# Score pairs first in the scheduling order, turned weights in small rotating tiles, a third raw weight buffer

## Chip, cores and metric

One core of a Trainium2 chip runs the kernel. The metric is the device time of one execution in microseconds; the number to predict is the median of the runs of the changed kernel.

## What is computed

Two transformer blocks of two layers each, one after the other, in float32, on 512 tokens of width 1024. The first block's layer has two attention mixers on one input projection, gates, an output projection, and a gated feed-forward with a short convolution. The second block has a chunked linear attention, a differential attention, a Fourier mixer and a gated feed-forward, on the tokens and on 256 context tokens. The change touches the first block's two mixers in code, and the weight loads of everything.

```python
# mixer A, per head: windows in three groups of heads (dilation 1, 4, 16)
scores = einsum(q, k) * hd ** -0.5 + alibi bias, masked
p = exp(scores - max);  o = (p @ v) / sum(p)
# mixer B (stick-breaking), per block of 128 queries
z = einsum(q_blk, k) * hd ** -0.5
log_stay = where(causal, log_sigmoid(-z), 0)
later = reverse_cumsum(log_stay) - log_stay
o = where(causal, exp(log_sigmoid(z) + later), 0) @ v
```

Heads have 64 dimensions. Mixer A has three groups of four heads, mixer B four heads.

## The kernel before, in words

The program is traced in Python through a tile framework. Each engine gets its instructions in an order that a planner fixes when the program is built: it takes what is ready by its own time model, the earliest in program order first. Tiles come from pools with a number of buffers for each tag; who wants a buffer that is still in use waits for its last reader.

**Weights.** `weights` (line 106) hands out a weight and asks for the one that the next call will want. `load_weights` (line 116) takes, for each 128 x 1024 piece, a raw tile (pool "raw", two buffers, line 55), a high-half tile (three buffers) and a low-half tile (two), issues the load on the SP queue (line 125), casts raw to the high half on ACT (line 126) and subtracts it from raw on DVE (line 127). So a raw buffer is free when the subtraction is done. Every projection (`mm3`, lines 133 to 135) is three matmuls a piece: high by high, high by low, low by high. A piece feeds 24 matmuls of 512 columns for the tokens, or of 256 columns for the context or half the tokens.

**The two mixers of the first block** (`mixer1`): q, k and v are projected; then for j = 0 and 1 `stick` (line 541) and `dsw` (line 472) are traced, then the joining of the groups, 16 gate projections, and the output. The planner puts matmuls of the gate projections between the attention's.

A head pair shares tiles: head 0 has partitions 0 to 63 of q and k, head 1 has 64 to 127, and each has its own bank in a score tile `sc` of two banks (one such tile).

- `stick`, for each of four query blocks: scores of the pair (line 553, 128 to 512 columns), tanh on ACT (555), mask, stay factors, two scans and a product on DVE (557 to 565), `turned`, then the value products (570). There the two heads write different halves of the partitions of `po`.
- `dsw`, for each of four blocks: scores for three groups of heads (line 488), bias and maximum on DVE (494) and exp on ACT (496) for each head and half, `turned`, the value products (505), and copies of sums (508, 509).
- `turned` (line 459) turns the weights of both heads by 128 x 128 transposes into one tile `at` of two banks (line 467) and copies them to SBUF by `evac`: head 0 on ACT (line 785), head 1 on DVE (line 783). The target is one pair tile `pT` with one buffer.

`self.tmp` gives tiles of 128 x 512 from the pool "tmp" with four buffers; the first block uses it before attention (squares of x) and after it (joining, merging, feed-forward).

Of the kernel before, what the change touches and what calls it, by code (L numbers as in the profile page):

```python
# [18 lines left out]
P = 128  # L19
# [11 lines left out]
class Split:  # L31


    def __init__(self, hi, lo):
        self.hi, self.lo = hi, lo
# [12 lines left out]
class Net:  # L48
    def __init__(self, ctx, tc, io, plan):
        self.plan, self.asked, self.ahead = plan, [], []  # L50
        self.tc, self.nc, self.io = tc, tc.nc, io
        pool = lambda name, bufs, **kw: ctx.enter_context(tc.tile_pool(name=name, bufs=bufs, **kw))
        self.pc = pool("const", 1)
        self.px = pool("resid", 1)
        self.praw = pool("raw", 2)
        self.pw = pool("wsplit", 1)
        self.ps = pool("tmp", 4)
        self.psm = pool("small", 4)
        self.n = 0
        self.consts()  # L60
# [398 lines left out]
    def turned(self, t, n):  # L459

        nc = self.nc
        pt = self.pair_bank("at")
        pT = self.pair_tile("pT")
        for i in range(2):
            for k in range(n):
                sl = slice(k * P, (k + 1) * P)
                nc.tensor.transpose(pt[:, i, sl], t[:, i, sl], self.ident)
        for i in range(2):
            self.evac(i, pT[:, i, :n * P], pt[:, i, :n * P])
        return pT  # L470

    def dsw(self, j, qa, ka, va, sums, stat):

        nc = self.nc
        bias = self.pair_tile("bias")
        nc.sync.dma_start(bias, self.io["dswb"][2 * j:2 * j + 2].rearrange("s p c -> p s c"))
        for b in range(4):
            k0 = max(b - 1, 0) * P  # L480
            n0 = (b + 1) * P - k0
            own = slice(b * P, (b + 1) * P)
            ps = self.pair_bank("sc")
            for g, cols, keys in ((0, slice(0, n0), slice(k0, (b + 1) * P)), (1, slice(n0, n0 + P), own),
                                  (2, slice(n0 + P, n0 + 2 * P), own)):
                for i in range(2):
                    r = slice(64 * i, 64 * i + 64)
                    nc.tensor.matmul(ps[:, i, cols], qa[2 * g + j][r, own], ka[2 * g + j][r, keys], start=True, stop=True)
            e = self.pair_tile("y", 2)
            for i in range(2):  # L490
                s = 2 * j + i
                for c, (sl, bi) in enumerate(((slice(0, n0), slice(256 - n0, 256)), (slice(n0, n0 + 2 * P), slice(256, 512)))):
                    nm = stat[:, c, b, 0, s:s + 1]
                    nc.vector.tensor_tensor_reduce(e[:, i, sl], ps[:, i, sl], bias[:, i, bi], -1.0, 3.0e38, ALU.add, ALU.min,
                                                   accum_out=nm)
                    nc.scalar.activation(e[:, i, sl], e[:, i, sl], AF.Exp, bias=nm, scale=-1.0)
            n = n0 // P + 2
            pT = self.turned(e, n)
            po = self.bank("po")
            for i in range(2):  # L500
                s = 2 * j + i
                vs = [(0, va[0][k0 // P + k][:, s, :]) for k in range(n - 2)]
                vs += [(1, va[1][b][:, 4 * (g - 1) + s, :]) for g in (1, 2)]
                for k, (c, v) in enumerate(vs):
                    nc.tensor.matmul(po[:, 130 * i + 65 * c:130 * i + 65 * (c + 1)], pT[:, i, k * P:(k + 1) * P], v,  # L505
                                     start=k in (0, n - 2), stop=k in (n - 3, n - 1))
            po = po[:, 0:260].rearrange("p (s c d) -> p c s d", s=2, c=2)
            nc.scalar.copy(sums[b][:, :, 2 * j:2 * j + 2, :], po[:, :, :, 0:64])
            nc.vector.tensor_copy(stat[:, :, b, 1, 2 * j:2 * j + 2], po[:, :, :, 64])
# [31 lines left out]
    def stick(self, j, qb, kb, vb):  # L541

        nc = self.nc
        po = self.bank("po")
        for qi in range(4):
            kw = (qi + 1) * P
            pz = self.pair_bank("sc")  # L550
            for i in range(2):
                r = slice(64 * i, 64 * i + 64)
                nc.tensor.matmul(pz[:, i, :kw], qb[j][r, qi * P:kw], kb[j][r, 0:kw], start=True, stop=True)
            y = self.pair_tile("y", 2)
            nc.scalar.activation(y[:, :, :kw], pz[:, :, :kw], AF.Tanh, scale=0.5)
            d = y[:, :, qi * P:kw]
            nc.vector.tensor_tensor(d, d, self.smask.unsqueeze(1).broadcast_to([P, 2, P]), ALU.min)

            g = self.pair_tile("stay")
            nc.gpsimd.memset(g[:, :, 0:1], 1.0)  # L560
            nc.vector.tensor_scalar(g[:, :, kw - 1:0:-1], y[:, :, 1:kw], -0.5, 0.5, ALU.mult, ALU.add)
            for i in range(2):
                c = g[:, i, 0:kw]
                nc.vector.tensor_tensor_scan(c, c, c, 1.0, ALU.mult, ALU.bypass)
            nc.vector.scalar_tensor_tensor(y[:, :, :kw], y[:, :, :kw], 1.0, g[:, :, 0:kw][:, :, ::-1], ALU.add, ALU.mult)
            pT = self.turned(y, qi + 1)
            for k in range(qi + 1):
                for i in range(2):
                    h = 2 * j + i
                    nc.tensor.matmul(po[64 * i:64 * i + 64, qi * P:kw], vb[:, k, h * 64:(h + 1) * 64], pT[:, i, k * P:(k + 1) * P],  # L570
                                     start=k == 0, stop=k == qi, tile_position=(0, 64 * i))
        o = self.pv.tile([P, T], F32, tag=f"ob{j}", name=self.nm("ob"))
        nc.scalar.copy(o, po)
        return o
# [1111 lines left out]
```

## Time and profile before

| | us |
|---|---|
| median of three runs | 3280.42 |
| lowest and highest run | 3278.43, 3285.65 |
| the profiled execution | 3286.37 |
| its span, first to last instruction | 3284.6 |
| PE busy in it | 3200.1 |
| DVE, ACT busy in it | 2000.4, 1350.6 |

PE is TensorE's matmul, DVE is VectorE, ACT is ScalarE, SP the engine that issues most loads. A busy PE is not a PE at its peak: matmuls are pipelined, so a record lasts longer than the distance from one start to the next. A float32 matmul shows as two records, a projection matmul as one. "mm<-h,whi" names what an instruction writes and reads. A row of the timeline merges consecutive records of one line and operation and shows their count; the time in it runs from the start of the first to the end of the last. What stands behind an arrow is the instruction that ended the idle time before.

### The profile page before, as it was taken

Reading aid. Unit: us, or ns where it says so; the run is one execution under the profiler, and the core shown is the slowest. Engines: PE = TensorE matmul, PEld = TensorE weight load, DVE = VectorE, ACT = ScalarE, POOL = GpSimd, SP = SyncE. Lnnn points to the kernel's source line nnn. Section 1 sums busy time; section 2 is a strip of 40 time slices with the busy share of each in tenths; the row PEclk is TensorE's granted clock in tenths of the full one; section 3 lists DMA queues with packets and bytes.
Section 4 is the critical chain, followed back from the end, with each engine's and each line's share of the span. In section 5 each row is a group of like instructions: output and inputs, shape, how many; then the busy total and the mean of one; then the engine's idle time right before and its main releaser. Section 6 shows DMA issues by size and latency. Waiting matters only on the chain.

```text
span 3284.6 us, 46618 instructions
## 1 busy us (share of the span) xinstructions
PE 3200.1 (97%) x18792; PEld 2674.0 (81%) x18792; DVE 2000.4 (61%) x3256; ACT 1350.6 (41%) x2246; POOL 68.8 (2%) x197
## 2 busy tenths in 40 slices
PE   9999999999999999999999999999999999999997
PEld 7778887888778887888778788888898778888887
DVE  4456799663556899567767765333266677652335
ACT  3243432242243423346647644222235467542223
POOL 0000000000000000000100000000000100000000
PEclk9999999999999999999999999999999999999999
DMA  4213466432223566344332134332134522223333
GB/s 133 84 40 119 145 199 209 124 103 91 70 81 94 162 210 199 118 133 151 101 115 70 58 118 133 93 99 85 58 117 128 166 77 70 78 78 96 96 96 116
DMA packets 109159, 370.59 MB, mean 113 GB/s; under 512 B 13200, under 2 KB 18320, under 8 KB 108944
## 3 DMA queue, kind: packets, MB, share of 16 engines
q1 hardware_dynamic: 103760, 352.28, 35.0%
q0 software_dynamic: 5184, 15.34, 1.6%
q8 instruction: 147, 2.41, 0.3%
q14 instruction: 68, 0.56, 0.1%
HBM read 359.64 MB, written 7.93 MB: 112 GB/s over the span
## 4 chain that ended last, share of the span: by engine, by line
PE 73%; DVE 11%; DMA 10%; ACT 4%; issue 1%; ACTq 0%; SPq 0%; DVEq 0%
PE mm L135 19%; PE mm L133 19%; PE mm L134 19%; DVE wlo L127 3%; DMA raw<-w_up 3%; ACT whi L126 2%; DVE junk L689 2%; DMA raw<-w_fi 2%; DMA wmod<-w_mod 1%; DVE wmod L689 1%; PE at L1273 1%; DMA raw<-w_in2t 1%; DMA raw<-w_fo 1%; PE po L505 1%; DMA raw<-w_in2v 1%
## 5 line engine op out<-in xcount | busy, mean ns | idle before, releaser
L126 ACT CAST whi<-raw 128x1024 fp32r<-128x1024 f32 (+1 forms) x556 | 576.0, 1036 | 1282.3 <-PE mm L134 282.7
L127 DVE TENSOR_TENSOR wlo<-raw,whi 128x1024 fp32r<-128x1024 f32 (+1 forms) x556 | 667.2, 1200 | 364.2 <-PE mm L135 170.7
L133 PE MATMUL mm<-h,whi 128*128 128x512 f32 x1904 | 753.0, 396 | 13.6 <-ACT whi L126 6.9
L135 PE MATMUL mm<-h,wlo 128*128 128x512 f32 x1904 | 753.6, 396 | 1.1 <-DVE wlo L127 0.9
L134 PE MATMUL mm<-h,whi 128*128 128x512 f32 x1904 | 751.0, 394 | 0.0
L133 PEld LDWEIGHTS mm<-h,whi 128*128 128x128 f32 x1904 | 358.8, 188 | 88.3 <-ACT whi L126 10.0
L135 PEld LDWEIGHTS mm<-h,wlo 128*128 128x128 f32 x1904 | 358.5, 188 | 79.9 <-DVE wlo L127 7.3
L134 PEld LDWEIGHTS mm<-h,whi 128*128 128x128 f32 x1904 | 358.7, 188 | 72.6 <-issue 2.8
L135 PE MATMUL mm<-hid,wlo 128*128 128x512 f32 (+1 forms) x896 | 325.7, 364 | 4.0 <-DVE wlo L127 3.7
L133 PE MATMUL mm<-hid,whi 128*128 128x512 f32 (+1 forms) x896 | 324.4, 363 | 1.8 <-ACT whi L126 1.8
L134 PE MATMUL mm<-hid,whi 128*128 128x512 f32 (+1 forms) x896 | 324.1, 362 | 0.9 <-DVE hid L180 0.9
L135 PEld LDWEIGHTS mm<-hid,wlo 128*128 128x128 f32 x896 | 168.0, 188 | 35.3 <-DVE wlo L127 7.6
L133 PEld LDWEIGHTS mm<-hid,whi 128*128 128x128 f32 x896 | 168.0, 188 | 29.7 <-ACT whi L126 2.0
L134 PEld LDWEIGHTS mm<-hid,whi 128*128 128x128 f32 x896 | 168.1, 188 | 29.0 <-DVE hid L180 1.4
L133 PE MATMUL mm<-cat,whi 128*128 128x512 f32 (+1 forms) x512 | 185.9, 365 | 3.2 <-ACT cat L716 2.7
L135 PE MATMUL mm<-cat,wlo 128*128 128x512 f32 (+1 forms) x512 | 186.2, 364 | 0.2 <-DVE wlo L127 0.2
L134 PE MATMUL mm<-cat,whi 128*128 128x512 f32 (+1 forms) x512 | 185.7, 363 | 0.0
L1414 DVE TENSOR_TENSOR silu<-silu,mm 128x512 f32<-128x512 f32 (+1 forms) x58 | 36.1, 623 | 221.6 <-PE mm L135 221.1
L689 DVE SCALAR_TENSOR_TENSOR junk<-wmod,c 128x1024 f32<-128x1024 f32 x96 | 116.8, 1217 | 4.2 <-DMA wmod<-w_mod 3.7
L689 DVE SCALAR_TENSOR_TENSOR wmod<-wmod,c 128x1024 f32<-128x1024 f32 x96 | 116.8, 1217 | 0.7
L133 PEld LDWEIGHTS mm<-cat,whi 128*128 128x128 f32 x512 | 96.2, 189 | 18.8 <-ACT cat L716 2.9
L135 PEld LDWEIGHTS mm<-cat,wlo 128*128 128x128 f32 x512 | 96.4, 189 | 15.4 <-DVE wlo L127 0.4
(491 smaller groups left out, 5119.5 us busy)
## 6 DMA issues: line engine op xcount, KB each, us to landing
raw<-w_fi SPq DMA_DIRECT2D x120, 512.0 KB, 3.6
wmod<-w_mod SPq DMA_DIRECT2D x96, 512.0 KB, 4.2
raw<-w_up SPq DMA_DIRECT2D x88, 512.0 KB, 3.7
raw<-w_in2t SPq DMA_DIRECT2D x76, 512.0 KB, 3.7
raw<-w_in_t SPq DMA_DIRECT2D x64, 512.0 KB, 3.6
raw<-w_fo SPq DMA_DIRECT2D x48, 512.0 KB, 3.5
raw<-w_down SPq DMA_DIRECT2D x32, 512.0 KB, 3.7
raw<-w_out SPq DMA_DIRECT2D x28, 512.0 KB, 3.6
```

What stands on the lines that cost most here:

```text
L126: nc.scalar.copy(hi, raw)
L127: nc.vector.tensor_tensor(lo, raw, hi.bitcast(F32), ALU.subtract)
L133: mm(out, lh, rh, start=start, stop=False)
L134: mm(out, lh, rl, start=False, stop=False)
L135: mm(out, ll, rh, start=False, stop=stop)
L505: nc.tensor.matmul(po[:, 130 * i + 65 * c:130 * i + 65 * (c + 1)], pT[:, i, k * P:(k + 1) * P], v, start=k in (0, n - 2), stop=k in (n - 3 ...
L689: ins = nc.vector.scalar_tensor_tensor(o, w, 1.0, cs[v], ALU.mult, ALU.mult, accum_out=self.mods[l][v][:, j:j + 1])
L1273: mm(po[:, 0:64], wT[:, i * P:(i + 1) * P], vals[c0 + i][:, h * 64:(h + 1) * 64], start=c0 + i == 0, stop=c0 + i == nkb - 1)
L1414: nc.vector.tensor_tensor(s, s, ps[1][:, :n], ALU.mult)
```

## The change

Three edits. The score matmuls in `stick` and `dsw` are traced inside `high_priority()`, which gives them the priority of the program's start, so that the planner takes them before anything else that is ready. `turned` copies each head's turned weights into a tile of its own from `tmp`; the value products of `stick` take head 1 before head 0. The raw pool has three buffers.

```diff
--- before.py
+++ after.py
@@ -52,7 +52,7 @@
         pool = lambda name, bufs, **kw: ctx.enter_context(tc.tile_pool(name=name, bufs=bufs, **kw))
         self.pc = pool("const", 1)
         self.px = pool("resid", 1)
-        self.praw = pool("raw", 2)
+        self.praw = pool("raw", 3)
         self.pw = pool("wsplit", 1)
         self.ps = pool("tmp", 4)
         self.psm = pool("small", 4)
@@ -460,13 +460,13 @@
 
         nc = self.nc
         pt = self.pair_bank("at")
-        pT = self.pair_tile("pT")
+        pT = [self.tmp("pT") for _ in range(2)]
         for i in range(2):
             for k in range(n):
                 sl = slice(k * P, (k + 1) * P)
                 nc.tensor.transpose(pt[:, i, sl], t[:, i, sl], self.ident)
         for i in range(2):
-            self.evac(i, pT[:, i, :n * P], pt[:, i, :n * P])
+            self.evac(i, pT[i][:, :n * P], pt[:, i, :n * P])
         return pT
 
     def dsw(self, j, qa, ka, va, sums, stat):
@@ -483,9 +483,10 @@
             ps = self.pair_bank("sc")
             for g, cols, keys in ((0, slice(0, n0), slice(k0, (b + 1) * P)), (1, slice(n0, n0 + P), own),
                                   (2, slice(n0 + P, n0 + 2 * P), own)):
-                for i in range(2):
-                    r = slice(64 * i, 64 * i + 64)
-                    nc.tensor.matmul(ps[:, i, cols], qa[2 * g + j][r, own], ka[2 * g + j][r, keys], start=True, stop=True)
+                with self.tc.high_priority():
+                    for i in range(2):
+                        r = slice(64 * i, 64 * i + 64)
+                        nc.tensor.matmul(ps[:, i, cols], qa[2 * g + j][r, own], ka[2 * g + j][r, keys], start=True, stop=True)
             e = self.pair_tile("y", 2)
             for i in range(2):
                 s = 2 * j + i
@@ -502,7 +503,7 @@
                 vs = [(0, va[0][k0 // P + k][:, s, :]) for k in range(n - 2)]
                 vs += [(1, va[1][b][:, 4 * (g - 1) + s, :]) for g in (1, 2)]
                 for k, (c, v) in enumerate(vs):
-                    nc.tensor.matmul(po[:, 130 * i + 65 * c:130 * i + 65 * (c + 1)], pT[:, i, k * P:(k + 1) * P], v,
+                    nc.tensor.matmul(po[:, 130 * i + 65 * c:130 * i + 65 * (c + 1)], pT[i][:, k * P:(k + 1) * P], v,
                                      start=k in (0, n - 2), stop=k in (n - 3, n - 1))
             po = po[:, 0:260].rearrange("p (s c d) -> p c s d", s=2, c=2)
             nc.scalar.copy(sums[b][:, :, 2 * j:2 * j + 2, :], po[:, :, :, 0:64])
@@ -548,9 +549,10 @@
         for qi in range(4):
             kw = (qi + 1) * P
             pz = self.pair_bank("sc")
-            for i in range(2):
-                r = slice(64 * i, 64 * i + 64)
-                nc.tensor.matmul(pz[:, i, :kw], qb[j][r, qi * P:kw], kb[j][r, 0:kw], start=True, stop=True)
+            with self.tc.high_priority():
+                for i in range(2):
+                    r = slice(64 * i, 64 * i + 64)
+                    nc.tensor.matmul(pz[:, i, :kw], qb[j][r, qi * P:kw], kb[j][r, 0:kw], start=True, stop=True)
             y = self.pair_tile("y", 2)
             nc.scalar.activation(y[:, :, :kw], pz[:, :, :kw], AF.Tanh, scale=0.5)
             d = y[:, :, qi * P:kw]
@@ -565,9 +567,9 @@
             nc.vector.scalar_tensor_tensor(y[:, :, :kw], y[:, :, :kw], 1.0, g[:, :, 0:kw][:, :, ::-1], ALU.add, ALU.mult)
             pT = self.turned(y, qi + 1)
             for k in range(qi + 1):
-                for i in range(2):
+                for i in (1, 0):
                     h = 2 * j + i
-                    nc.tensor.matmul(po[64 * i:64 * i + 64, qi * P:kw], vb[:, k, h * 64:(h + 1) * 64], pT[:, i, k * P:(k + 1) * P],
+                    nc.tensor.matmul(po[64 * i:64 * i + 64, qi * P:kw], vb[:, k, h * 64:(h + 1) * 64], pT[i][:, k * P:(k + 1) * P],
                                      start=k == 0, stop=k == qi, tile_position=(0, 64 * i))
         o = self.pv.tile([P, T], F32, tag=f"ob{j}", name=self.nm("ob"))
         nc.scalar.copy(o, po)
```

## Rows read from the trace of the kernel before

**Rows 1.** Part 1 of the page: busy time, share of the span and instructions of each engine.
```profile
PE 3200.1 (97%) x18792; PEld 2674.0 (81%) x18792; DVE 2000.4 (61%) x3256; ACT 1350.6 (41%) x2246; POOL 68.8 (2%) x197
```
**Rows 2.** Windows: stretch, busy us (xinstructions) by engine, granted clock, DMA share, GB/s.
```profile
145.00:235.00 90.00, 88.07 (x543) 62.67 (x542) 54.92 (x138) 36.89 (x72) 3.84 (x11) 1.00 0.11 33
866.00:956.00 90.00, 87.90 (x536) 62.37 (x535) 54.58 (x138) 36.89 (x72) 2.98 (x9) 0.98 0.11 32
1930.00:2010.00 80.00, 76.55 (x611) 73.69 (x609) 63.65 (x95) 43.93 (x65) 0.00 (x0) 0.98 0.50 152
2050.00:2100.00 50.00, 50.00 (x222) 41.36 (x221) 16.79 (x20) 14.73 (x20) 0.00 (x0) 1.00 0.31 95
```
**Rows 3.** Groups by line, 145 to 235 us: busy us, mean ns, then idle before and releaser.
```profile
L488 PE MATMUL sc<-qk,qk 64*128 64x128 f32 (+1 forms) x96 | 14.4, 334 | 0.0
L494 DVE CUSTOM_DVE_ANT_0 y<-sc,bias 128x256 f32<-128x256 f32 (+1 forms) x32 | 11.4, 401 | 7.3 <-PE sc L488 7.3
L553 PE MATMUL sc<-qk,qk 64*128 64x128 f32 (+3 forms) x32 | 10.8, 482 | 0.3 <-ACT y L555 0.3
L783 DVE COPY pT<-at 128x512 f32<-128x512 f32 (+3 forms) x16 | 9.1, 570 | 14.8 <-ACT pT L785 14.7
L570 PE MATMUL po<-pT,vb 128*64 128x128 f32 x80 | 8.7, 286 | 0.7 <-DVE pT L783 0.5
```
**Rows 4.** Timeline of PE, 145 to 201 us: start, us, operation, merged records.
```profile
145.98 0.49 PE L553 MATMUL sc<-qk,qk 64*128 64x128 f32 x4
...
149.26 0.70 PE L553 MATMUL sc<-qk,qk 64*128 64x256 f32 x4 [0.29 <-ACT y L555]
...
152.56 0.44 PE L570 MATMUL po<-pT,vb 128*64 128x128 f32 x4
...
152.92 0.91 PE L553 MATMUL sc<-qk,qk 64*128 64x384 f32 x2
...
155.33 1.12 PE L553 MATMUL sc<-qk,qk 64*128 64x512 f32 x2
...
156.38 0.66 PE L570 MATMUL po<-pT,vb 128*64 128x128 f32 x8
...
160.53 0.43 PE L570 MATMUL po<-pT,vb 128*64 128x128 f32 x2
...
191.97 0.92 PE L553 MATMUL sc<-qk,qk 64*128 64x384 f32 x4
...
199.90 0.94 PE L488 MATMUL sc<-qk,qk 64*128 64x128 f32 x12
```
**Rows 5.** Waits of PE, whole run: line, releaser, us in total, times, longest us.
```profile
PE mm L135 <- DVE wlo L127: 12.8, 27, 1.1
PE mm L133 <- ACT whi L126: 12.7, 6, 6.9
PE mm L171 <- DVE wlo L127: 3.5, 5, 0.8
PE mm L153 <- DVE wlo L127: 2.1, 1, 2.1
PE mm L170 <- ACT whi L126: 1.5, 3, 0.8
PE sc L553 <- ACT y L555: 0.7, 2, 0.4
```
**Rows 6.** Timeline of DVE, 1946 to 1957 us.
```profile
1949.12 1.22 DVE L127 TENSOR_TENSOR wlo<-raw,whi 128x1024 fp32r<-128x1024 f32 x1 [0.80 <-ACT whi L126]
...
1955.14 1.22 DVE L127 TENSOR_TENSOR wlo<-raw,whi 128x1024 fp32r<-128x1024 f32 x1 [0.30 <-ACT whi L126]
```
**Rows 7.** Timeline of PE in the same stretch.
```profile
1950.98 0.28 PE L133 MATMUL mm<-KK,whi 128*128 128x256 f32 x1
...
1951.33 0.28 PE L133 MATMUL mm<-KK,whi 128*128 128x256 f32 x1
```
**Rows 8.** DMA issues: count, size of one, median us from issue to landing.
```profile
raw<-w_fi SPq DMA_DIRECT2D x120, 512.0 KB, 3.6
```

## The prediction

> **What bounds the kernel now.** I read the share of busy time first: PE is busy 97% of the span, DVE 61%, ACT 41% [rows 1]. So whatever does not shorten the instruction stream of PE, or remove a moment in which PE stands, is worth nothing. Busy is no throughput, though, so the windows come next [rows 2]. In a dense projection stretch (2050 to 2100 us) PE runs 222 matmuls of 512 columns in 50 us, one every 0.225 us, without a gap and at the full granted clock; nothing in this change touches that rate, and dense stretches make up most of the kernel. Two kinds of stretch differ.
>
> The first kind is attention in the two layers of the first block, 145 to 235 us and 866 to 956 us. PE is busy 88.07 and 87.90 of 90 us there, DVE 54.9 and 54.6, so PE is the bound [rows 2]. But what PE does is wasteful. The scores of two heads lie in the two halves of the partitions (0 to 63 and 64 to 127). Where both matmuls of a pair stand next to each other, the timeline shows them running at the same time: four records of 384 columns take 0.92 us, while two records of one head alone take 0.91 us [rows 4]. Many pairs are torn apart by transposes or value products of the step before, which come earlier in the program and so win as soon as they are ready. Then each half pays the full price.
>
> The second kind is where the weight chain is late: the second block's stages that work on 256 columns, 1930 to 2010 us for one, where PE is busy 76.55 of 80 us [rows 2]. The waits of PE say what it stands for: the high or low half of a weight [rows 5].
>
> **The change part by part.**
>
> *Score pairs with priority.* No instruction is added or removed; the order on PE's queue changes. I take what each line costs PE now in one attention stretch and what it would cost with every pair whole, from the merged records [rows 3, 4]. Stick-breaking scores (L553): four sizes per half, paired 0.49 + 0.70 + 0.92 + 1.12 = 3.23 us (the last is the row of one head, since at 384 columns one and two cost the same), twice 6.46; now 10.8, so 4.3 us less. Window scores (L488): three pairs of 128 columns take 0.94 us, and a block whose first pair has 256 columns takes 0.21 more (0.70 less 0.49), so 2 x (0.94 + 3 x 1.15) = 8.8; now 14.4, so 5.6 us less. Value products of the stick part (L570) use two column halves in the same way; the loop order (1, 0) starts with the head that DVE evacuates last, so that a pair is not begun with one member. Two records of one head and four of both cost the same there, 0.43 and 0.44 us, eight take 0.66 [rows 4]: with 0.22 for each further pair, 2 x (0.44 + 0.66 + 0.88 + 1.10) = 6.2; now 8.7, so 2.5 us less. Together 12.4 us per layer and 24.8 us for both, if PE stays the bound. It will not stay so everywhere. When 12 of 90 us vanish, steps that ACT and DVE do (tanh, scans, evacuation) become the last to arrive now and then, and the projections that fill gaps have places fixed at build time. The two ends are 0 and 24.8. I take two thirds, 16.5 us: PE at 98% against DVE at 61% is nearer to the full end.
>
> What the scores are moved past: transposes and value products of the step before, each up to one score set later (1.15 us), so that step's evacuation is later too. The next scores then find their bank free, and projections cover the shift; I price it at nothing, and without that cover it is the rival of in-order waiting below.
>
> *Turned weights in the small tiles.* Same copies, same matmuls, two separate tiles from a pool of four instead of one pair tile. A step's copies need no longer wait for the value products of the step before. The row to read is DVE's copy: it idles 14.8 us per layer, 14.7 of it put down to ACT's copy of the other head [rows 3]. If the shared tile is what orders the two, that goes; if the order comes from the shared transpose bank, it stays. DVE is not the bound, so between 0 and 29.4 us of idle time I take a twentieth, 1.5 us. The pool's other users in this stage come before or after attention, so nobody waits for these tiles. What the change frees, 4 KB a partition, is what the third raw buffer needs.
>
> *A third raw buffer.* Nothing is computed anew; a load may be issued when the third last subtraction is done, not the second last. In dense stretches a weight lasts 24 x 0.225 = 5.4 us and the loads are ahead: worth 0. In 256-column stages three matmuls start every 0.35 us, a weight lasts 2.8 us [rows 7]. The chain of one buffer is load, cast, subtract, next load: the subtractions of every second weight start 6.02 us apart, at 1949.12 and 1955.14 [rows 6], so two buffers deliver a weight every 3.0 us, too slow by 0.2. Three would deliver one per 2.0 us, and PE becomes the bound again. The landing itself is 3.6 us [rows 8]. How much is there to win in all? The five large groups of waits of PE for a half weight sum to 12.8 + 12.7 + 3.5 + 2.1 + 1.5 = 32.6 us [rows 5]; 6.9 of that is the wait for the very first weight, which stays: 25.7. I take two thirds, 17 us, since in the first load after a stage border, and where the low half has just two buffers, another wait is behind it. The ends are 4 us (only the steady 0.2 us on some twenty weights) and 25.7. On SP's queue the earlier loads go past loads of context, masks and consts, whose users are later; there I price nothing, and if they come late it is a part of the third that I left out.
>
> The Trainium skill speaks against this part: its page "DMA: Bandwidth & Descriptors", section "Anatomy of one DMA", gives a fixed 2.0 us plus bytes over 436 GB/s (fitted on GpSimd's path). By it, as an estimate, 512 KB would land in 3.2 us, two buffers would give a weight about every 2.8 us, just PE's own pace, and this part would be worth close to 0, which is rival B. The measured landing of 3.6 us and the measured spacing of 6.02 us differ from it, so the sum goes by the rows.
>
> *Sum.* 16.5 + 1.5 + 17 = 35 us. The profiled execution took 3286.4 us (span 3284.6), 6.0 above the median of the runs; 35 less is 3251 there, and 3245 against the median of 3280.4.
>
> **Rivals.**
> *A, the pairs are whole but the time is given back*: the ACT and DVE steps behind each score become the bound, PE idles as much as it saved. For it: the chain of a stick step is serial; against it: DVE has 35 of 90 us free. Only 17 + 1.5 us remain: 3262.
> *B, the third buffer changes little*: weights are then held by the two low-half buffers, or by loads that share bandwidth. For it: most waits of PE name the low half, written last [rows 5]; against it: a landing of 3.6 us [rows 8] and a subtraction of 1.22 us [rows 6] already make up 4.8 of the 6.02 us, and the cast stands between them. 16.5 + 1.5 us remain: 3262.
> *C, in-order waiting, slower*: a score with top priority is queued as soon as the planner thinks its bank is free. If the bank's readers are late on the chip, the score stands at the head of PE's queue with transposes, value products and projections behind it: at 149.26 us PE stands 0.29 us before a score [rows 4], though a projection follows that needs nothing of it. Today such a wait is seen twice, 0.7 us in all [rows 5]; from above it is bounded by the four reductions that empty a bank, 11.4 us over 8 blocks or 1.43 us [rows 3]. There are 32 score sets in the two layers: at 1.43 us each 46 us, 11 more than the gains, so 3291. It cancels the gain at 1.1 us a set.
> The Trainium skill, page "TensorE: Matmul & The Clock Gate", section "Packing small matmuls", states that matmuls start and end strictly in order, which is the rule by which C would come.
> *D, the change does not do what it says*: members of a pair still become ready at different times and stay apart, and loads keep their places: 3280.
>
> **How the numbers follow.** Forecast (both parts work) 0.57, A 0.14, B 0.12, D 0.08, C 0.09. The predicted time is the forecast's, 3245. With all gains at their upper ends (24.8 + 25.7, and 7.5 for DVE's copies, a quarter of their idle time) it would be 3222; with the pairing at 4 and the buffer at 4 us 3272. That holds the forecast, A and B, and leaves out C and D, 0.17 in all. A measurement of this kernel tells about 0.2% (6.6 us) from no change. Faster by more: forecast, A and B, 0.83. Within: D, 0.08. Slower: C, 0.09.
>
> **What would show it.** Right: in the timeline scores come as four records (stick) or twelve (window) without anything between; L553 near 6.5 us and L488 near 8.8 us per attention stretch; the stretch from first stick score to the last value product shorter by some 8 us per layer; waits of PE for half weights near 15 us instead of 32.6; subtractions in 1940 to 1980 us every 2.8 us. Wrong: L553 and L488 unchanged (D); shorter score lines with new idle time of PE before transposes or value products (A); waits of PE at the score lines of tens of us (C); waits for the low half as before (B).

## The result, and the profile after

The changed kernel takes 3232.66 us (median of four runs, 3230.16 to 3236.54) against 3280.17 us of the kernel before in the same measurement: ratio 0.9853, 95% interval 0.9836 to 0.9870. That is 47.5 us less. The forecast was 3245, 35 us less; the result lies inside the range (3222 to 3272) and in its faster part. Measured once more on another chip the ratio was 0.9825 (0.9812 to 0.9839).

The profiled execution took 3236.54 us. Span and busy time, from the page of the changed kernel:

```profile
span 3234.8 us, 46579 instructions
...
PE 3159.5 (98%) x18792; PEld 2665.4 (82%) x18792; DVE 1997.6 (62%) x3256; ACT 1344.3 (42%) x2244; POOL 68.1 (2%) x197
```

PE has the same 18792 matmuls as before [rows 1] and is busy 40.6 us less: 50 us of span are gone, so some 9 us of idle PE went as well.

Line numbers have moved by one or two: the scores are L489 (windows) and L555 (stick), the value products L506 and L572, the copies of turned weights L785 (DVE) and L787 (ACT). Windows of the changed kernel: the first attention stretch, the stretch of the second block that had been 1930 to 2010 us, and a dense one (columns as in [rows 2]):

```profile
145.00:235.00 90.00, 85.11 (x590) 67.81 (x589) 59.90 (x152) 43.35 (x83) 3.80 (x11) 1.00 0.19 58
1887.00:1967.00 80.00, 78.99 (x639) 76.78 (x637) 64.46 (x96) 46.24 (x68) 0.00 (x0) 1.00 0.53 164
2005.00:2055.00 50.00, 50.00 (x222) 41.39 (x221) 16.34 (x18) 14.89 (x19) 0.00 (x0) 1.00 0.30 95
```

In 145 to 235 us PE runs 590 matmuls where it ran 543, with 3 us less busy time. 12 score records have moved out of the stretch (three groups of four; the timeline below has the first), so there are 59 more projections, 59 x 0.225 = 13 us of later work. In the second row 639 matmuls stand where 611 stood in the same 80 us; the 28 more are matmuls of 512 columns (31 where 3 stood), which were later work before. The dense row has not changed: 222 in 50 us.

The score and value lines in the groups by line, over the whole run (so two attention stretches, while [rows 3] has one):

```profile
L489 PE MATMUL sc<-qk,qk 64*128 64x128 f32 (+1 forms) x192 | 17.5, 315 | 0.0
...
L572 PE MATMUL po<-pT,vb 128*64 128x128 f32 x160 | 14.0, 286 | 8.8 <-DVE pT L785 8.8
...
L555 PE MATMUL sc<-qk,qk 64*128 64x128 f32 (+3 forms) x64 | 13.0, 482 | 0.0
```

And DVE's copies of turned weights in the same view:

```profile
L785 DVE COPY pT<-at 128x512 f32<-128x512 f32 (+3 forms) x32 | 18.2, 570 | 15.9 <-ACT pT L787 15.8
```

Window scores 8.75 us a layer (forecast 8.8), stick scores 6.5 (forecast 6.5), value products 7.0 (forecast 6.2). DVE idles 8 us a layer before its copies instead of 14.8, and still because of ACT's copy. PE timeline, to be held against [rows 4]:

```profile
32.68 0.49 PE L555 MATMUL sc<-qk,qk 64*128 64x128 f32 x4
...
150.10 1.13 PE L555 MATMUL sc<-qk,qk 64*128 64x512 f32 x4
...
154.94 0.43 PE L572 MATMUL po<-pT,vb 128*64 128x128 f32 x2 [1.36 <-DVE pT L785]
155.30 0.94 PE L489 MATMUL sc<-qk,qk 64*128 64x128 f32 x12
```

All six window scores of a block are now one group of twelve records, and two heads of 512 columns take 1.13 us where one head took 1.12. The first stick scores are not even in the attention stretch: they run at 32.68 us, among the value projections, as soon as their operands are there. The row at 154.94 shows the new price: a value product at the head of PE stands for DVE's copy. It also shows a pair of value products still torn: two records, then the twelve scores, and the other six from 156.17 us. The last value products of `dsw` in the first layer start at 216.15 us, where they started at 229.80; the prediction's sign of a stretch some 8 us shorter can't be read as it was meant, since the first stick scores have left the stretch. The waits of PE, as in [rows 5]:

```profile
PE po L572 <- DVE pT L785: 8.8, 10, 1.4
PE mm L133 <- ACT whi L126: 7.5, 2, 7.2
PE mm L135 <- DVE wlo L127: 4.5, 4, 1.9
...
PE mm L153 <- DVE wlo L127: 1.7, 2, 1.3
...
PE mm L170 <- ACT whi L126: 0.9, 1, 0.9
...
PE mm L171 <- DVE wlo L127: 0.8, 1, 0.8
```

The five half-weight groups sum to 7.5 + 4.5 + 1.7 + 0.9 + 0.8 = 15.4 us (32.6 before; forecast near 15). No score line is among the waits. In their place L572 waits 8.8 us for DVE. And the subtractions, to be held against [rows 6], follow at PE's pace:

```profile
1919.49 1.22 DVE L127 TENSOR_TENSOR wlo<-raw,whi 128x1024 fp32r<-128x1024 f32 x1
...
1922.26 1.22 DVE L127 TENSOR_TENSOR wlo<-raw,whi 128x1024 fp32r<-128x1024 f32 x1
...
1924.97 1.22 DVE L127 TENSOR_TENSOR wlo<-raw,whi 128x1024 fp32r<-128x1024 f32 x1
```

They are 2.77 and 2.71 us apart, where two weights took 6.02 us.

### The profile page after: what moved, and what is told of

It reads as the page before. It is cut to its first block, busy times and chain, and to the rows that moved or that the text cites. A ratio compares the mean times of both kernels' runs of the same rounds, so it can differ in the third digit from the quotient of the medians.

```text
span 3234.8 us, 46579 instructions
## 1 busy us (share of the span) xinstructions
PE 3159.5 (98%) x18792; PEld 2665.4 (82%) x18792; DVE 1997.6 (62%) x3256; ACT 1344.3 (42%) x2244; POOL 68.1 (2%) x197
## 4 chain that ended last, share of the span: by engine, by line
PE 88%; DVE 5%; ACT 3%; DMA 2%; issue 1%; SPq 0%; DVEq 0%; ACTq 0%
PE mm L133 24%; PE mm L135 24%; PE mm L134 24%; PE at L1275 2%; DVE wlo L127 1%; ACT whi L126 1%; PE mm L171 1%; PE po L506 1%; PE mm L172 1%; PE mm L170 1%; PE ds L1253 1%; PE at L1271 1%; PE lev L1157 1%; PE lev L1103 1%; DVE stay L566 1%
```

## Experiments

Runs that were measured together share a chip and its runs of the kernel before; medians of that kernel differ from chip to chip (3280 to 3289 us), so ratios are compared. A ratio is not the quotient of the two medians: in the first three runs below it gives 2 to 3 us more than they do.

**The priority alone.** The kernel before, with this edit and nothing else:

```diff
-                for i in range(2):
-                    r = slice(64 * i, 64 * i + 64)
+                with self.tc.high_priority():
+                    for i in range(2):
+                        r = slice(64 * i, 64 * i + 64)
...
```

> The kernel before with the score priority alone (two raw buffers, one pair tile for the turned weights, value products from head 0). Theory, whole pairs are what the priority gives: L553 and L488 fall by some 8 to 9 us per layer and the time by 17 to 24 us, to 3256 to 3263. Rival, the priority needs the separate tiles and the new order to pay: 3270 to 3280.

Measured 3271.8 us, ratio 0.9951 (0.9934 to 0.9968), 13.5 us less than the 3285.3 of that chip; by the ratio 16 us (10.5 to 21.7 by its interval). The theory's 17 to 24 lies partly inside that interval; the rival's range, 0 to 10 us less, lies just outside. Groups by line, whole run:

```profile
L572 PE MATMUL po<-pT,vb 128*64 128x128 f32 x160 | 19.1, 287 | 3.7 <-DVE pT L785 2.5 <-ACT pT L787 1.3
...
L489 PE MATMUL sc<-qk,qk 64*128 64x128 f32 (+1 forms) x192 | 17.5, 315 | 0.0
...
L555 PE MATMUL sc<-qk,qk 64*128 64x128 f32 (+3 forms) x64 | 13.0, 482 | 0.0
```

The score lines fall from 28.7 + 21.6 to 17.5 + 13.0 us, 19.8 less, just what the working had (9.9 a layer). Value products of the stick part get longer with the old loop order: 19.1 instead of 17.4 us, and the timeline shows scores and transposes between their halves (at 163 to 168 us, for one). So the priority pays without the rest.

Where it pays can be read at the 5000th matmul of PE, in the output projection behind the second layer's attention: in both kernels and in the runs named with it below the same matmuls stand before it. In the timelines of the kernel before, of this run, and of the changed kernel with two raw buffers (the next run) it is

```profile
1079.94 0.39 PE L133 MATMUL mm<-merged,whi 128*128 128x512 f32 x1
...
1056.90 0.39 PE L133 MATMUL mm<-merged,whi 128*128 128x512 f32 x1
...
1056.08 0.39 PE L133 MATMUL mm<-merged,whi 128*128 128x512 f32 x1
```

Up to there the priority alone is 23.0 us ahead and the changed kernel with two raw buffers 23.9, nearly the full 24.8 (the granted clock, 0.98 in the second stretch of the kernel before [rows 2], is at most 1.8 us of it). At the end of the spans 18.4 and 16.8 us are left. So 4.6 and 7.1 us are lost in the rest of the run, which the priority does not touch. The run of the separate tiles alone, which gains nothing, loses 3.6 us there too, so a good part of the loss is the spread between executions; whether there is more to it is not shown.

**The changed kernel with two raw buffers.**

```diff
-        self.praw = pool("raw", 3)
+        self.praw = pool("raw", 2)
```

> The changed kernel with two raw buffers. Theory, the two parts add up: the second block's gain of some 17 us and the few us of the feed-forward stages go, 3252 to 3257, and the waits of PE for half weights are back near 30 us. Rival B, the third buffer changes little: 3233 to 3238. Rival, nearly everything is the buffer: 3265 to 3275.

Measured 3270.98 us, ratio 0.9950 (0.9935 to 0.9966): 14.3 us less than before (16 by the ratio, 11 to 21 by its interval), where the theory had 23 to 28; the range of the rival that nearly everything is the buffer (3265 to 3275) holds the time. The waits of PE for half weights are back as forecast, at [rows 5]'s size:

```profile
PE mm L133 <- ACT whi L126: 15.5, 7, 7.9
PE mm L135 <- DVE wlo L127: 14.1, 28, 1.4
```

So the third buffer is worth more than was thought: with it the ratio is 0.9853, without it 0.9950.

**The third buffer without priority.** The changed kernel with the score blocks and the order of the value products as before:

```diff
-                with self.tc.high_priority():
...
-                for i in (1, 0):
+                for i in range(2):
```

> The changed kernel without the priority and with the value products from head 0: a third raw buffer, and the separate tiles that make room for it. Theory: 3254 to 3262, that is 18 to 26 us less than before, and score lines as long as before. Rival B: 3275 to 3282. Rival, the buffer is nearly everything: 3238 to 3245.

Measured 3254.55 us, ratio 0.9897 (0.9879 to 0.9915): 30.7 us less (34 by the ratio, 28 to 40 by its interval), above the theory's 18 to 26 and far from rival B. The two largest half-weight waits of PE:

```profile
PE mm L133 <- ACT whi L126: 8.2, 2, 7.8
PE mm L135 <- DVE wlo L127: 3.5, 3, 1.9
```

and the stretch that had been 1930 to 2010 us, as a window:

```profile
1910.00:1990.00 80.00, 78.68 (x637) 76.39 (x636) 65.45 (x97) 46.24 (x68) 0.00 (x0) 1.00 0.53 165
```

With L171 (0.8), L153 (1.9) and none on L170 the five groups sum to 14.4 us, 18.2 less than before, while the time fell by 30.7. The window says why idle time is too small a price: PE's busy time rose only from 76.55 to 78.68 us, by 2.1, but its matmuls from 611 to 637, and the 26 more are all of 512 columns. At 0.225 us each that is 5.9 us of later work; the granted clock, 1.00 here and 0.98 before, is at most 1.6 us of it. A starved PE looks busy, because each record lasts longer than its place in the stream: 0.28 us against 2.8 / 24 = 0.12 us at 256 columns [rows 7], so a start that is up to 0.16 us late shows no idle time.

The traces bear this out over the whole run. Take every projection matmul of 256 or 512 columns that follows another, outside the stretches at the lower granted clock, and add up by how much its start is later than the steady distance (0.118 and 0.227 us): 89.6 us in the kernel before, 62.4 in this run, 27.2 less. The idle time of PE before the same matmuls is 34.5 and 22.5 us, only 12.0 less.

**The separate tiles alone.** The kernel before with

```diff
-        pT = self.pair_tile("pT")
+        pT = [self.tmp("pT") for _ in range(2)]
...
-            self.evac(i, pT[:, i, :n * P], pt[:, i, :n * P])
+            self.evac(i, pT[i][:, :n * P], pt[:, i, :n * P])
```

> The kernel before with the separate small tiles alone (two raw buffers, no priority, value products from head 0). Theory: within 3 us of before, 3277 to 3283, and DVE's copy still starts when ACT's copy of the other head ends. Rival, the shared target tile held DVE back: 3268 to 3275, and DVE's copy starts before ACT's has ended.

Measured 3288.53 us, ratio 1.0008 (0.9996 to 1.0019): no difference. DVE's copies:

```profile
L783 DVE COPY pT<-at 128x512 f32<-128x512 f32 (+3 forms) x32 | 18.3, 571 | 31.4 <-ACT pT L785 31.1
```

They wait for ACT's as before (29.4 us in both layers from [rows 3]). So the shared target did not order the copies, and the edit's use is the room that it makes for the raw buffer. The shorter wait of the changed kernel (15.9) comes from the priority: in the run with that alone it is 13.8 us.

**One bank per head for the transposes**, in the changed kernel:

```diff
-        pt = self.pair_bank("at")
+        pt = [self.bank("at") for _ in range(2)]
...
-                nc.tensor.transpose(pt[:, i, sl], t[:, i, sl], self.ident)
+                nc.tensor.transpose(pt[i][:, sl], t[:, i, sl], self.ident)
...
-            self.evac(i, pT[i][:, :n * P], pt[:, i, :n * P])
+            self.evac(i, pT[i][:, :n * P], pt[i][:, :n * P])
```

(The pool has two buffers of one bank each instead of one of two.)

> The changed kernel with one bank per head for the transposes instead of one tile of two banks. Theory, the shared transpose tile is what orders DVE's copy behind ACT's: DVE's copies now start before ACT's end, the waits of PE for them shrink, and the time falls by 2 to 8 us, 3225 to 3231. Rival, something else orders them: copies as before and 3231 to 3235.

Measured 3231.11 us, ratio 0.9826 (0.9810 to 0.9842). DVE's copies:

```profile
L785 DVE COPY pT<-at 128x512 f32<-128x512 f32 (+3 forms) x32 | 18.1, 567 | 7.1 <-PE at L467 5.5 <-ACT ob L575 1.7
```

Now they wait for the transposes (5.5 us) and no longer for the other head's copy. That the shared transpose tile ordered the two copies is shown. It is worth no time that can be told: the changed kernel's own ratios are 0.9853 and 0.9825. (At the 5000th matmul this one trace is 2.9 us ahead of the changed kernel's first one; the theory's 2 to 8 us is neither shown nor ruled out at its lower end.)

**Window scores of one head, then of the other**, under the same priority:

```diff
-            for g, cols, keys in (...):
-                with self.tc.high_priority():
-                    for i in range(2):
+            with self.tc.high_priority():
+                for i in range(2):
+                    for g, cols, keys in (...):
```

> The changed kernel with the window scores of one head issued before those of the other (the same six matmuls under the same priority). Theory, the gain is the two heads at the same time: L489 rises from about 8.5 to 12 to 14 us of PE per layer, the time by 6 to 10 us, to 3239 to 3243. Rival, the priority itself (earlier scores) is the gain: within 2 us of the changed kernel.

Measured 3237.20 us, ratio 0.9844 (0.9829 to 0.9859), 6 us more than the two other variants with three raw buffers on its chip (3230.65 and 3231.11). The intervals of the ratios overlap, but the traces place the difference: at the 5000th matmul this run is 20.9 us ahead of the kernel before, the changed kernel 26.9 and, in its second trace, 27.3. Groups by line:

```profile
L489 PE MATMUL sc<-qk,qk 64*128 64x128 f32 (+1 forms) x192 | 25.2, 315 | 0.0
```

The same matmuls, equally early, take 25.2 instead of 17.5 us, 7.7 more. So of the window scores' part of the gain most is concurrency, not the earlier place.

**Value products from head 0 again**, in the changed kernel, on two chips:

```diff
-                for i in (1, 0):
+                for i in range(2):
```

> The changed kernel with the value products of the stick part from head 0 again. Theory, starting with the head that is copied last keeps pairs whole: slower by 2 to 4 us than the changed kernel, 3235 to 3237, and L572 back near 8.7 us per stretch. Rival, the new order makes PE stand for DVE's copy (8.8 us of waits in the changed kernel): faster by 2 to 6 us, 3227 to 3231.

> The changed kernel with the value products of the stick part from head 0, beside the changed kernel on one chip. Theory after the first run of it: the whole pairs that the new order gives (5 us less on L572) are paid back in waits for DVE's copy (5 us more), so the two are within 5 us of each other. Rival: the old order is better by 6 us or more.

Measured 3230.65 us, ratio 0.9823 (0.9808 to 0.9838), and 3231.54 us, 0.9826 (0.9812 to 0.9839). From the first:

```profile
L572 PE MATMUL po<-pT,vb 128*64 128x128 f32 x160 | 19.1, 287 | 3.5 <-DVE pT L785 3.5
```

Busy time of the line is 5.1 us higher than with the new order (14.0), the idle time before it 5.3 lower (3.5 for 8.8). The new order makes more pairs whole and pays for it by standing for DVE; nothing that can be told is left over, and both lie with the changed kernel.

**The changed kernel again**, beside the variants.

> The changed kernel once more, on the chip of the three that follow, as their measure. Ratio to the kernel before as in the first measurement, 0.983 to 0.987.

Measured 3230.59 us, ratio 0.9825 (0.9812 to 0.9839).

**One bank per head and head 0 first.**

> One transpose bank per head, and the value products from head 0. Theory: DVE's copies no longer wait for ACT's, and the product of head 0 need not wait for DVE: 3 to 8 us faster than the changed kernel on this chip. Rival: PE is the bound all the same and the time is within 3 us of the changed kernel.

Measured 3229.33 us, ratio 0.9816 (0.9803 to 0.9829): 1.3 us less than the changed kernel on the same chip, inside the interval. The rival holds: PE is the bound all the same. No version here beats the changed kernel beyond noise.

**A third low-half buffer in place of the third raw buffer.**

```diff
-        self.praw = pool("raw", 3)
+        self.praw = pool("raw", 2)
...
-                               for t, b in (("whi", 3), ("wlo", 2))]
+                               for t, b in (("whi", 3), ("wlo", 3))]
```

> The changed kernel with the 4 KB of the third raw buffer given to a third low-half buffer. Theory, raw buffers are what is short: as with two raw buffers, 3250 to 3257. Rival B, low halves are short: 3230 to 3238.

Measured 3251.56 us. That lies in the theory's range, but the range does not fit its words: with two raw buffers the time had been 3271. The chip's kernel before took 3288.8: the ratio is 0.9888 (0.9871 to 0.9904) against 0.9950 with two of each. So the 4 KB bring some 20 us as a low-half buffer (0.0062 of 3285) and 32 to 41 us as a raw buffer (0.9950 against the changed kernel's 0.9853 and 0.9825). These are ratios from different chips, and the changed kernel's own two differ by 0.0028, 9 us, so the sizes are rough. The late starts, counted as above within each trace, give the same order: 86.3 us with two of each, 74.4 with the third low-half buffer, 56.7 in the changed kernel, so 12 us against 30. The theory that raw buffers alone are short falls; waits of PE for halves are between the two cases:

```profile
PE mm L133 <- ACT whi L126: 10.2, 4, 6.9
...
PE mm L135 <- DVE wlo L127: 6.8, 10, 1.5
```

Both extra buffers at once were not tried.

**One raw buffer.**

```diff
-        self.praw = pool("raw", 3)
+        self.praw = pool("raw", 1)
```

> The changed kernel with one raw buffer. Theory, load, cast and subtraction of one buffer follow each other in 6.0 us: with one buffer every weight takes 6.0 us, also in the dense stretches (5.4 us of PE each), so about 0.6 us more on some 400 weights and 3.3 us on some 150, 3700 to 4000 us in all. Rival, loads are not chained through the buffer: below 3400.

Measured 3959.8 us in one run, inside the theory's 3700 to 4000. Subtractions in a dense stretch:

```profile
304.83 1.23 DVE L127 TENSOR_TENSOR wlo<-raw,whi 128x1024 fp32r<-128x1024 f32 x1
...
311.13 1.22 DVE L127 TENSOR_TENSOR wlo<-raw,whi 128x1024 fp32r<-128x1024 f32 x1
...
317.26 1.22 DVE L127 TENSOR_TENSOR wlo<-raw,whi 128x1024 fp32r<-128x1024 f32 x1
...
323.50 1.22 DVE L127 TENSOR_TENSOR wlo<-raw,whi 128x1024 fp32r<-128x1024 f32 x1
```

With one buffer a weight comes every 6.1 to 6.3 us, the same length that two buffers shared in [rows 6]; PE needs 5.4. The cycle of load, cast and subtraction belongs to the buffer and not to the load path. The total is a looser match: the mean granted clock of this run is 0.937 (0.90 from 2000 to 3000 us, where PE is busy 874 of 1000 us), and the theory's sum had no clock in it, so that it comes so near is partly luck.

## Why the prediction was right, point by point

- **What bounds the kernel**: right. PE's dense rate is untouched, and the variants that only free DVE or ACT (separate tiles, one bank per head) are worth nothing that can be told.
- **Score pairs**: the working of the full gain was right to a few tenths for the scores (19.8 us measured, 19.8 worked out) and too high for the value products (3.4 instead of 5.0). The value products came short at least in part because some pairs are still torn: the set at 154.94 us takes 0.43 and 0.65 us in two pieces, where eight records in one take 0.66 [rows 4]. Of the 24.8 us I took 16.5; the priority alone gave 13.5 us, and the changed kernel with two raw buffers, which has the new loop order too, 14.3 (both 16 by the ratio). So the number fits, but not for the reason given. ACT and DVE steps do arrive last now and then: PE idles 3 us more in the first attention stretch, and L572 stands 8.8 us for DVE's copies. Yet behind the second attention 23.0 and 23.9 us are gained, so these waits cost little of it; most of what is missing at the end is lost in later stages that the edit does not touch (4.6 and 7.1 us, where a run without any gain loses 3.6). That two thirds came out is in part luck.
- **Turned weights in the small tiles**: 1.5 us was taken, none was found (ratio 1.0008). Of the two causes that were left open for DVE's wait, the shared transpose bank tile was it.
- **The third raw buffer**: the mechanism was right, the size was the step that failed. The waits for half weights fell by 17.2 us, from 32.6 to 15.4, as taken (17), and the subtractions run at PE's pace (the first load's wait stays, 7.2 us). But the time fell by 30.7 us in the run with the buffer and without priority. The mis-sized term is "two thirds of 25.7 us": the idle time that is booked to a releaser is no upper end for a starved stretch. The count of matmuls would have been a better one: of the 611 in the stretch of 80 us, 576 have 256 columns, 67.2 us at 2.8 us for 24; three of 512 columns and 32 small ones take some 5.4 us more. So up to 7.4 us were to be won there and not the 3.45 us in which PE was idle; 5.9 us came.
- **The landing time**: the Trainium skill's page "DMA: Bandwidth & Descriptors", section "Anatomy of one DMA", would have had this part at nearly nothing (3.2 us a load, as an estimate); its fit is for loads issued by GpSimd, and these are issued by SP. The run with the third buffer and the one with a single buffer speak for the row's 3.6 us and the 6.02 us cycle; the measurement decides.
- **Rivals.** B (the third buffer changes little) is out by its own run. But its reason, too few low-half buffers, is half true: a third one of these alone is worth some 20 us. A did not come: behind the second attention 23 of the 24.8 us are still there. D is out by the timeline. C did not come at the scores: L489 and L555 have no idle time before them. Something like it came at another place: the value product of the head that is copied last stands in order for its copy, 8.8 us in all. The rule of the Trainium skill, page "TensorE: Matmul & The Clock Gate", section "Packing small matmuls", that matmuls keep their order, agrees with that row: PE stands 1.36 us at 154.94 us, and the scores come after.

The sum of the parts holds within the intervals: 13.5 us (priority) and 30.7 us (buffer, tiles) are 44 us, by the ratios 16 and 34 are 50, against 47.5 and 48 for the whole. The whole is 12 us above the 35 that were forecast, and nearly all of that is the third buffer.

## What to carry to other kernels

A pair of matmuls on two halves of the partitions is worth what the merged records say only if nothing comes between them: read in the timeline how many records stand together, price them by the rows of whole pairs, and give the pair one priority. Price a starved stretch by its matmuls times their steady distance, not by the idle time of the engine. For a chain of load and conversions, divide the cycle of one buffer by the number of buffers and compare with the time the consumer needs; a buffer count that is just short costs in every weight.

## What the runs showed of the hardware that was not expected

Two float32 matmuls of 512 columns on the two halves of the partitions take 1.13 us together, while one took 1.12 us: at this size, too, the second head costs nothing. And a load of 512 KB gains nothing by being alone. With one raw buffer at most one load into a raw buffer is under way, yet it lands in the median after 3.6 us, as with two buffers [rows 8]. DMA issues of that run, in the view of [rows 8]:

```profile
raw<-w_fi SPq DMA_DIRECT2D x120, 512.0 KB, 3.6
```

So a second load in flight costs the first one nothing that this median shows; if it did, another buffer would bring less.
